# Stick-breaking attention: causal masks added ahead of the logits, and one pair of squares held behind an exponential

## The chip, the cores and the metric

The kernel runs on one core of one Trainium2 chip. The metric is the device time of one execution in microseconds (us), as the median of several runs. TensorE (PE in the profile) multiplies matrices, with its weight loads shown apart as PEld; VectorE is DVE, ScalarE is ACT, GpSimd is POOL, SyncE is SP.

## The reference

Four layers work on 256 tokens of 1024 features. Each adds a token mixer and then a squared-ReLU MLP to the residual, both on an RMS-normed input. The mixers are retention (layers 0 and 3), a convolution module (layer 1) and stick-breaking attention (layer 2). Only the last is touched by the change. Cut to what matters:

```python
q, k, v = split(xn @ w_in, 3)               # 16 heads of 64; q and k are RMS-normed per head
for b0 in range(0, s, SB_BLOCK):            # two query blocks of 128
    kend = b0 + SB_BLOCK
    z = einsum('bhqd,bhkd->bhqk', q[:, :, b0:kend], k[:, :, :kend]) * scale
    mask = s_idx[None, :] < t_idx[:, None]  # strictly causal
    log_1mb = where(mask, log_sigmoid(-z), 0.0)
    log_w = log_sigmoid(z) + cumsum(log_1mb, reverse=True) - log_1mb
    a = where(mask, exp(log_w), 0.0)
    outs.append(einsum('bhqk,bhkd->bhqd', a, v[:, :, :kend]))
y = concatenate(outs) @ w_out
```

## The kernel before

Weights stream from memory all the time. Each unit of 128x1024 numbers is split into a rounded high part (`wh`, a cast on ScalarE, line 350) and the rest (`wl`, a subtraction on VectorE, line 357), and products are summed from high and low parts in PSUM. Most of the kernel is a long row of such matmuls.

In the attention layer (`stick`), the 16 heads go in four blocks of four heads. TensorE's order is written out by hand in the string `SB_ORDER`, one short code for a step; the digit that follows is the block:

- `p` (`proj`): a quarter of the block's q and k projection, 12 matmuls of 512 columns (lines 918 to 920); `r`: the row norms; `v` (`values`): a quarter of a v projection, of the same shape.
- `n` (`norm`): per-head norms. ScalarE squares the two projected tiles out of PSUM (line 1372), VectorE sums them (line 1374), takes an inverse root (lines 384 to 395) and scales the tiles (line 1384).
- `u` and `t` (`trans`): four TensorE transposes of q, or of k (line 1394), into one PSUM tile `pt`, which ScalarE copies out (line 1399; for q also two copies of half of the rows, line 1406).
- `l` (`logits`): three PSUM tiles z2, z0, z1. Four matmuls for z2 (line 1420; keys of the second half against queries of the second half), the mask of z2 (line 1427), four matmuls for z0 and z1 (line 1433; their operands lie on 64 rows), then the masks of z0 and z1 (also line 1427). A mask is a matmul of an identity with a matrix that holds -1e30 in the places that are cut off, so it is added in PSUM.
- `s` (`soft`): per tile, absolute value, exponential and logarithm on ScalarE (lines 1445 to 1447), then three operations on VectorE (lines 1448 to 1451).
- `w` (`weights`): `w02` stands for block 0, tile z2. Suffix sums are added to the tile by TensorE (lines 1458 and 1462), and ScalarE takes the exponential of the tile (line 1464). That is the last reader of the tile.
- `m` (`mix`): the attention weights against v.

The small PSUM tiles (the `pt` of every transpose step, and z2, z0, z1) share a pool of four banks, `mis`. A step that wants a bank waits until an earlier tile's last reader is done; TensorE takes its steps strictly in the written order, so such a wait holds up everything behind it.

The part of the order that matters here is:

```python
"p00 p01 r p02 p03 p10 n0 p11 p12 p13 u0 t0 p20 n1 l0 s0 p21 p22 w02 p23 n2 w00 u1 t1 p30 l1 p31 p32 s1"
" w01 w12 p33 w10 u2 t2 w11 v00 n3 l2 s2 v01 v02 w22 v03 u3 t3 w20 v10 l3 v11 s3 w21 v12 w32 v13 w31 w30"
```

Only TensorE keeps this order. The orders of ScalarE, VectorE and GpSimd within the layer are laid out by a planner at build time, which lists the instructions by its own estimates of time and urgency; each engine then runs its list from first to last.

Of the kernel before, what the change touches and what calls it, by code (L numbers as in the profile page):

```python
# [2 lines left out]

# [8 lines left out]
AF = mybir.ActivationFunctionType  # L12
# [3 lines left out]
P = 128  # L16
D = 1024
S = 256
# [220 lines left out]
def v3(ap, a, b):  # L239
    return ap.rearrange("p (a b) -> p a b", a=a, b=b)  # L240


class Trunk:
# [1097 lines left out]
    def stick(self, j, nxt):  # L1341
        nc = self.nc
        self.table("natural_log_exp_and_others")
        kw = dict(skip_group_check=True)
        Ur, m1r, idr, negr = (self.cp.tile([P, P], F32R, name=f"{k}r", tag=f"{k}r") for k in ("U", "m1", "id", "neg"))
        for t, key in ((Ur, "U"), (m1r, "m1"), (idr, "id"), (negr, "neg")):
            nc.vector.tensor_copy(t, self.c(key, P))
        G = {}
# [17 lines left out]
        def norm(b):  # L1366
            pss = G["p", b]

            m = self.col(16, "qkm")
            for t in range(2):  # L1370
                sq = self.tmp()
                nc.scalar.activation(out=sq, in_=pss[t], func=AF.Square)
                ss = self.col(8, f"sbs{t}")
                nc.vector.tensor_reduce(out=ss, in_=v3(sq, 8, DH), op=ALU.add, axis=AX.X)
                nc.vector.tensor_scalar(
                    out=m[:, t * 8 : t * 8 + 8], in0=ss, scalar1=G["r64"][:, t : t + 1], scalar2=EPS,
                    op0=ALU.mult, op1=ALU.add,
                )
            rs = self.rsqrt(m, 16, "qk")
            f = self.col(16, "sbf")  # L1380
            nc.vector.tensor_mul(v3(f, 4, 4), v3(rs, 4, 4), G["rr"].unsqueeze(2).to_broadcast([P, 4, 4]))
            for t in range(2):
                sc = self.tmp()
                nc.vector.tensor_mul(
                    v3(sc, 8, DH), v3(pss[t], 8, DH), f[:, t * 8 : t * 8 + 8].unsqueeze(2).to_broadcast([P, 8, DH])
                )
                G["sc", b, t] = sc
# [23 lines left out]
        def logits(b):  # L1411


            z2, z0, z1 = self.mis(), self.mis(), self.mis()
            zb = G["z", b] = [z0, z1, z2]
            kT, qT = G["k", b], G["q", b]
            for e in range(2):
                for pr in range(2):
                    o = (2 * e + pr) * P
                    nc.tensor.matmul(  # L1420
                        zb[2][:, o : o + P], kT[:, pr * S + P : (pr + 1) * S], G["f", b][:, o : o + P],
                        start=o == 0, stop=False, **kw,
                    )

            def mask(z):
                n = z.shape[1]
                nc.tensor.matmul(z, idr, negr.unsqueeze(1).to_broadcast([P, n, P]), start=False, stop=True, **kw)

            mask(v3(zb[2], 4, P))
            for pr in range(2):  # L1430
                for e in range(2):
                    r = slice(e * DH, (e + 1) * DH)
                    nc.tensor.matmul(
                        zb[e][:, pr * S : (pr + 1) * S], kT[r, pr * S : pr * S + P], qT[r, pr * S : (pr + 1) * S],
                        start=pr == 0, stop=False, **kw,
                    )
            for e in range(2):
                mask(v3(zb[e], 2, S)[:, :, :P])

        def soft(b):  # L1440

# [12 lines left out]
        def weights(b, i):  # L1454

            zb = G["z", b]
            for x in G["l", b, i]:
                nc.tensor.matmul(zb[i], Ur, x, start=False, stop=True, **kw)  # L1458
            if i < 2:
                o = v3(zb[i], 2, S)[:, :, P:]  # L1460
                for x in G["l", b, 2]:
                    nc.tensor.matmul(o, m1r, v3(x[:, i * S : (i + 1) * S], 2, P), start=False, stop=True, **kw)
            G["A", b, i] = self.bigt()
            nc.scalar.activation(out=G["A", b, i], in_=zb[i], func=AF.Exp)

        def values(cb, kb):
            if kb == 0:
# [9 lines left out]
        def mix(b):  # L1477
# [15 lines left out]
        G["y"] = []  # L1493
        table = {
            "p": proj, "r": rnorm, "n": norm, "u": lambda b: trans(b, 0), "t": trans, "l": logits, "s": soft, "w": weights, "v": values, "m": mix
        }
        def go(steps):
# [62 lines left out]
```

## Time and profile before

| what | value |
| --- | --- |
| median of 3 runs | 1343.08 us (1341.48 to 1344.0) |
| span of the profiled execution | 1340.3 us |
| PE busy | 1330.8 us, 99% of the span |
| DVE, ACT, POOL busy | 984.0, 781.3, 134.0 us |
| PE clock granted | 9 in all 40 slices (90% or more); 1.00 in each stretch from 640 to 800 us |
| attention layer's blocks | about 668 to 756 us of the span |

The profile gives the profiled execution's span and no time of its own beside that; the span is 2.8 us below the median of the runs and 1.2 us below the fastest of them. In a timeline row the columns are the start, the length, the engine, the source line, the operation, the output and input tiles, the shapes and the number of merged instructions; the bracket names idle time ahead of it and what ended it. Matmul lengths overlap, since matmuls are pipelined: the distance between two starts is what one costs.

### The profile page before, as it was taken

How to read it: one execution, taken by the hardware profiler on the slowest of the kernel's cores; microseconds unless marked ns; L12 is line 12 of the kernel's file. 1: busy time of each engine (PE TensorE's matmuls, PEld its weight loads, DVE VectorE, ACT ScalarE, POOL GpSimd, SP SyncE). 2: the span in 40 equal slices, each digit the busy share in tenths (PEclk: the TensorE clock that was granted, in tenths of full speed). 3: DMA queues.
4: the chain of work that ended last, by engine and by line, in shares of the span. 5: the costliest groups of instructions: out<-in, count | busy, mean ns of one | idle time of the engine just before them, and what ended most of it. 6: DMA issues, size and time to landing. Idle time of an engine off the chain costs nothing.

```text
span 1340.3 us, 20902 instructions
## 1 busy us (share of the span) xinstructions
PE 1330.8 (99%) x8285; PEld 1170.4 (87%) x8285; DVE 984.0 (73%) x1642; ACT 781.3 (58%) x1205; POOL 134.0 (10%) x123
## 2 busy tenths in 40 slices
PE   9999999999999999999999999999999999999998
PEld 7988888888999998888878898888888888988886
DVE  6977769775688698765687587755697777788643
ACT  7555546664457477744578577744565555555442
POOL 3200002000169210000100010000120000100000
PEclk9999999999999999999999999999999999999999
DMA  7555555555545645555453345555555454555551
GB/s 283 210 184 190 187 181 197 189 188 189 188 159 145 219 170 203 190 192 192 172 183 126 126 166 190 192 190 194 177 181 187 174 188 173 189 189 189 204 188 63
DMA packets 41586, 244.56 MB, mean 182 GB/s; under 512 B 4624, under 2 KB 9104, under 8 KB 14096
## 3 DMA queue, kind: packets, MB, share of 16 engines
q1 hardware_dynamic: 40768, 240.86, 50.7%
q10 hardware_dynamic: 720, 2.36, 0.5%
q8 instruction: 65, 1.06, 0.3%
q14 instruction: 33, 0.27, 0.1%
HBM read 241.27 MB, written 1.93 MB: 181 GB/s over the span
## 4 chain that ended last, share of the span: by engine, by line
PE 99%; DMA 0%; ACT 0%; DVE 0%; issue 0%; SPq 0%
PE acc L524 34%; PE acc L520 18%; PE acc L683 6%; PE acc L918 6%; PE acc L920 6%; PE acc L919 6%; PE acc L504 4%; PE acc L505 4%; PE acc L506 4%; PE acc L1087 1%; PE acc L1220 1%; PE mis L809 1%; PE mis L870 1%; PE mis L400 0%; PE mis L1458 0%; PE acc L585 0%
## 5 line engine op out<-in xcount | busy, mean ns | idle before, releaser
L357 DVE TENSOR_TENSOR wl<-raw,wh 128x1024 fp32r<-128x1024 f32 (+1 forms) x440 | 546.5, 1247 | 242.8 <-ACT wh L350 236.4
L350 ACT CAST wh<-raw 128x1024 fp32r<-128x1024 f32 (+1 forms) x440 | 456.5, 1042 | 353.1 <-PE acc L524 164.8
L524 PE MATMUL acc<-z,wh 128*128 128x512 f32 x1120 | 387.4, 392 | 0.0
L520 PE MATMUL acc<-z,wl 128*128 128x256 f32 x1120 | 310.2, 281 | 0.0
L524 PE MATMUL acc<-big,wh 128*128 128x512 f32 x864 | 298.8, 392 | 0.0
L524 PEld LDWEIGHTS acc<-z,wh 128*128 128x128 f32 x1120 | 208.3, 187 | 44.7
L520 PE MATMUL acc<-big,wl 128*128 128x256 f32 x864 | 238.5, 280 | 0.5 <-DVE t L568 0.5
L520 PEld LDWEIGHTS acc<-z,wl 128*128 128x128 f32 x1120 | 211.1, 189 | 1.7
L524 PEld LDWEIGHTS acc<-big,wh 128*128 128x128 f32 x864 | 161.0, 187 | 34.8
L520 PEld LDWEIGHTS acc<-big,wl 128*128 128x128 f32 x864 | 162.4, 189 | 2.3 <-DVE t L568 1.3
L918 PE MATMUL acc<-wh,z 128*128 128x512 f32 x352 | 138.0, 392 | 0.0
L920 PE MATMUL acc<-wh,z 128*128 128x512 f32 x352 | 137.3, 390 | 0.0
L919 PE MATMUL acc<-wl,z 128*128 128x512 f32 x352 | 137.2, 390 | 0.0
L455 POOL TENSOR_TENSOR t<-t,t 128x512 f32<-128x512 f32 x23 | 36.2, 1573 | 893.7 <-ACT t L450 850.6
L567 ACT COPY t<-acc 128x256 f32<-128x256 f32 x176 | 61.8, 373 | 100.6 <-PE acc L524 99.3
L568 DVE TENSOR_TENSOR t<-acc,t 128x256 f32<-128x256 f32 x176 | 69.1, 421 | 34.9 <-ACT t L567 34.8
L683 PE MATMUL acc<-wh,big 128*128 128x512 f32 x256 | 79.3, 390 | 0.0
L920 PEld LDWEIGHTS acc<-wh,z 128*128 128x128 f32 x352 | 66.1, 188 | 14.7 <-issue 0.8
L918 PEld LDWEIGHTS acc<-wh,z 128*128 128x128 f32 x352 | 66.1, 188 | 14.1 <-issue 0.8
L919 PEld LDWEIGHTS acc<-wl,z 128*128 128x128 f32 x352 | 66.1, 188 | 13.1
L504 PE MATMUL acc<-z,wh 128*128 128x256 f32 x256 | 72.5, 284 | 0.0
L505 PE MATMUL acc<-z,wh 128*128 128x256 f32 x256 | 72.4, 283 | 0.0
(259 smaller groups left out, 1813.0 us busy)
## 6 DMA issues: line engine op xcount, KB each, us to landing
raw<-in_w SPq DMA_DIRECT2D x214, 1024.0 KB, 4.8
raw<-in_w SPq DMA_DIRECT2D x8, 512.0 KB, 8.9
big<-in_gn SPq DMA_DIRECT2D x16, 256.0 KB, 5.2
raw<-hd SPq DMA_DIRECT2D x8, 263.0 KB, 4.8
raw<-hd SPq DMA_DIRECT2D x8, 131.5 KB, 3.6
x<-in_x SPq DMA_DIRECT2D x4, 256.0 KB, 6.3
wh<-in_w ACTq DMA_DIRECT2D x2, 512.0 KB, 6.4
wl<-in_w ACTq DMA_DIRECT2D x2, 512.0 KB, 8.5
```

The source lines that it names most:

```text
L350: nc.scalar.copy(hi[:, s], src[:, s])
L357: self.nc.vector.tensor_sub(lo[:, s], src[:, s], hi[:, s])
L504: nc.tensor.matmul(o, wh[:, kk, cs], ah, start=st, stop=False, **kw)
L505: nc.tensor.matmul(o, wh[:, kk, cs], al, start=False, stop=False, **kw)
L520: mm = nc.tensor.matmul(ps[m][:, :S], wl[:, kk, cs], a[:, :S], start=first and kk == 0, stop=False, **kw)
L524: nc.tensor.matmul(ps[m], wh[:, kk, cs], a, start=False, stop=last and kk == 3, **kw)
L567: nc.scalar.copy(o[:, s], ps[m][:, S:])
L568: nc.vector.tensor_add(o[:, s], ps[m][:, :S], o[:, s])
L683: self.tc.keep_in_program_order(nc.tensor.matmul(ps[t], l, r[:, kk], start=False, stop=kb * 2 + kk == 31 and n == 2, **kw))
L918: nc.tensor.matmul(ps[t], zh[:, s], wh[:, kk], start=k == 0, stop=False, skip_group_check=True)
L919: nc.tensor.matmul(ps[t], zh[:, s], wl[:, kk], start=False, stop=False, skip_group_check=True)
L920: nc.tensor.matmul(ps[t], zl[:, s], wh[:, kk], start=False, stop=k == 7, skip_group_check=True)
```

## The change

Two edits in the attention layer. In `logits`, the three mask matmuls of a block come first and open their PSUM banks (`start=True`), and the eight logit matmuls are added to them; before, the logits came first and the masks closed the groups. In `norm`, for block 2 alone, the two squares carry an ordering edge: they are placed on ScalarE behind the latest exponential that `weights` has traced. With the written order that is the one of `w02`. The edge is an order on one engine; it adds no wait on another engine.

```diff
@@ norm
             for t in range(2):
                 sq = self.tmp()
-                nc.scalar.activation(out=sq, in_=pss[t], func=AF.Square)
+                with self.tc.issue_after(G["e"]) if b == 2 else nullcontext():
+                    nc.scalar.activation(out=sq, in_=pss[t], func=AF.Square)
@@ logits
+            def mask(z):
+                n = z.shape[1]
+                nc.tensor.matmul(z, idr, negr.unsqueeze(1).to_broadcast([P, n, P]), start=True, stop=False, **kw)
+
+            mask(v3(z2, 4, P))
+            for e in range(2):
+                mask(v3(zb[e], 2, S)[:, :, :P])
             for e in range(2):
                 for pr in range(2):
...
-                        start=o == 0, stop=False, **kw,
+                        start=False, stop=False, **kw,
                     )
-
-            def mask(z):
-                n = z.shape[1]
-                nc.tensor.matmul(z, idr, negr.unsqueeze(1).to_broadcast([P, n, P]), start=False, stop=True, **kw)
-
-            mask(v3(zb[2], 4, P))
             for pr in range(2):
                 for e in range(2):
...
-                        start=pr == 0, stop=False, **kw,
+                        start=False, stop=False, **kw,
                     )
-            for e in range(2):
-                mask(v3(zb[e], 2, S)[:, :, :P])
@@ weights
-            nc.scalar.activation(out=G["A", b, i], in_=zb[i], func=AF.Exp)
+            G["e"] = nc.scalar.activation(out=G["A", b, i], in_=zb[i], func=AF.Exp).ins
```

More of the change, by code (lines that the diff above doesn't have):

```diff
@@ L1 @@
 import numpy as np
-from contextlib import ExitStack
+from contextlib import ExitStack, nullcontext
 import concourse.bass as bass
```

## The prediction

> **What bounds the kernel now.** I read the page first: its parts 1, 2 and 4.
>
> ```profile
> span 1340.3 us, 20902 instructions
> PE 1330.8 (99%) x8285; PEld 1170.4 (87%) x8285; DVE 984.0 (73%) x1642; ACT 781.3 (58%) x1205; POOL 134.0 (10%) x123
> ...
> PE 99%; DMA 0%; ACT 0%; DVE 0%; issue 0%; SPq 0%
> ```
>
> TensorE is busy for 1330.8 of 1340.3 us, and the chain that ends last is TensorE for 99%. So a change is worth what it takes from TensorE's own row of instructions, or from the 9.5 us in which TensorE stands still. Next I asked for what TensorE waits for, over the whole execution (us in total, times, longest us).
>
> ```profile
> PE mis L292 <- POOL t L270: 1.3, 1, 1.3
> PE mis L1394 <- ACT big L1464: 1.0, 1, 1.0
> PE acc L585 <- ACT wh L350: 0.6, 1, 0.6
> PE acc L520 <- DVE t L568: 0.5, 2, 0.2
> ```
>
> Only one wait lies in the attention layer: a transpose (line 1394) waits once, 1.0 us, for an exponential of line 1464. The timeline shows its place. Here are TensorE's transposes of block 1, the wait, and the stall-free pair of block 0 for comparison:
>
> ```profile
> 684.05 1.03 PE L1394 MATMUL mis<-cst,t 128*128 128x128 f32 x8
> 684.84 0.47 PE L918 MATMUL acc<-wh,z 128*128 128x512 f32 x1
> 685.15 0.39 PE L919 MATMUL acc<-wl,z 128*128 128x512 f32 x1
> ...
> 695.76 0.61 PE L1458 MATMUL mis<-big,Ur 128*128 128x512 f32 x2
> ...
> 699.62 0.60 PE L1394 MATMUL mis<-cst,t 128*128 128x128 f32 x4
> 701.21 0.66 PE L1394 MATMUL mis<-cst,t 128*128 128x128 f32 x4 [0.99 <-ACT big L1464]
> 701.63 0.47 PE L918 MATMUL acc<-wh,z 128*128 128x512 f32 x1
> ```
>
> Four transposes (u1) run at 699.62; the next four (t1) start only at 701.21. The chain of waits tells why, and ScalarE's own timeline shows what it did before:
>
> ```profile
> 699.13 0.60 ACT t L1372
> 699.73 0.93 ACT wh L350
> 700.66 0.51 ACT big L1464
> ...
> 701.21 0.66 PE mis L1394 x4
> ```
>
> ```profile
> 696.91 0.62 ACT L1447 ACTIVATE t<-t 128x512 f32<-128x512 f32 x1
> 698.45 1.28 ACT L1372 ACTIVATE t<-acc 128x512 f32<-128x512 f32 x2 [0.91 <-PE acc L920]
> 699.62 1.04 ACT L350 CAST wh<-raw 128x1024 fp32r<-128x1024 f32 x1
> 700.56 1.09 ACT L1464 ACTIVATE big<-mis 128x512 f32<-128x512 f32 x2
> 701.52 0.70 ACT L1399 ACTIVATE big<-mis,prm 128x512 f32<-128x512 f32 x1
> 702.09 0.95 ACT L1406 ACTIVATE big<-mis,prm 64x256 f32<-64x256 f32 x2
> 703.07 0.69 ACT L1399 ACTIVATE big<-mis,prm 128x512 f32<-128x512 f32 x1
> ```
>
> The pair at 700.56 is the exponentials of w02 and w00. The one of w02 had its input since TensorE finished line 1458 at 695.76 + 0.61 = 696.37, yet it stands behind the two squares of block 2 and a weight cast. The squares themselves waited 0.91 us for TensorE, so ScalarE stood idle from 697.53 to 698.45 with that exponential ready. TensorE went on 0.65 us into the pair, just as the first of the two was done; the second ends at 701.65, too late to be the releaser.
>
> **The change part by part. The edge.** Both squares of block 2 now stand behind the exponential of w02. In place of the 0.91 us of idleness there is one exponential; the pair takes 1.09 us and its first member about 0.60 of it, so it runs from about 697.53 to 698.13 and the squares start at 698.45 as before. The edge adds no cross-engine wait: the exponential needs w02, which TensorE runs ahead of the projection that the squares need. Behind the squares nothing becomes late; their block is transposed (u2) much later than its scaling ends:
>
> ```profile
> 704.62 1.29 DVE L1384 TENSOR_TENSOR t<-acc,sbf 128x512 f32<-128x512 f32 x2
> ...
> 717.14 1.04 PE L1394 MATMUL mis<-cst,t 128*128 128x128 f32 x8
> ```
>
> That is 11.2 us of cover from 705.91 to 717.14. The bank of z2 is then free at about 698.2, before u1 begins, and t1 follows u1 without a gap. Block 0 gives the price of eight transposes in a row: 684.84 - 684.05 = 0.79 us. Block 1 took 701.63 - 699.62 = 2.01 us. The stall is worth 2.01 - 0.79 = 1.22 us; the bracket says 0.99, since it counts from the modelled end of the last transpose. I take 1.2 and keep 1.0 as the other end.
>
> What is late next is l1, which wants the copies of q and k out of PSUM.
>
> ```profile
> 704.48 1.05 PE L1420 MATMUL mis<-big,big 128*128 128x128 f32 x8
> ...
> 704.67 1.05 ACT L350 CAST wh<-raw 128x1024 fp32r<-128x1024 f32 x1 [0.92 <-PE acc L920]
> ```
>
> TensorE reaches l1 at 704.48 - 1.2 = 703.28. ScalarE has one exponential fewer behind the cast, 701.65 - 701.16 = 0.49 us, so k is copied by 703.76 - 0.49 = 703.27. Logits first would just meet it. Masks first put three matmuls of z2, z0, z1 in front (some 0.23 + 2 x 0.12 = 0.47 us by the rates below); they need no q or k, only banks, and the last bank, that of t1, is wanted at about 703.28 + 0.35 = 703.63. So the stall does not come back there, by a margin of about 0.35 us. After l1 the same chain of ScalarE is started by TensorE's progress (the 0.92 above, "PE acc L920"), so it moves ahead with it.
>
> **The masks.** No matmul is added or removed, only moved. Block 0 in TensorE's and the weight loads' timelines:
>
> ```profile
> 687.67 1.05 PE L1420 MATMUL mis<-big,big 128*128 128x128 f32 x8
> 688.48 0.48 PE L1427 MATMUL mis<-negr,idr 128*128 128x512 f32 x1
> 688.89 1.13 PE L1433 MATMUL mis<-big,big 64*128 64x256 f32 x8
> 688.89 0.73 PEld L1433 LDWEIGHTS mis<-big,big 64*128 64x128 f32 x8 [0.24 <-issue]
> 689.95 0.30 PEld L1427 LDWEIGHTS mis<-negr,idr 128*128 128x128 f32 x2 [0.33 <-issue]
> 689.95 0.50 PE L1427 MATMUL mis<-negr,idr 128*128 128x256 f32 x2
> 690.29 0.39 PE L918 MATMUL acc<-wh,z 128*128 128x512 f32 x1
> 690.52 0.39 PE L919 MATMUL acc<-wl,z 128*128 128x512 f32 x1
> ```
>
> Start to start, the steady 512-column matmul costs 690.52 - 690.29 = 0.23, so a 256-column one about 0.12 (an estimate, half of it). The z2 mask costs 688.89 - 688.48 = 0.41, 0.18 too much; the pair of masks 690.29 - 689.95 = 0.34, 0.10 too much. Part of that is the first rounded-type (fp32r) matmul behind plain fp32 ones: after the transposes it costs 685.15 - 684.84 = 0.31, 0.08 too much. The rest goes with the weight loads that stood idle for "issue", at the borders between 128-row and 64-row operands. A block now has two entries from fp32 to fp32r (z2's mask, the mask pair) and two row borders (into and out of line 1433). Afterwards it has one entry (the first projection matmul behind line 1433) and still two borders: into line 1433 from line 1420, and out of it into the projection. So I take one entry saved in each block, 4 x 0.08 = 0.3 us. Best case, both excesses go: 4 x 0.28 = 1.1 us gained. Worst case, no entry is saved and a border is dearer, by 0.33 - 0.24 = 0.09 as the two idle loads differ: 4 x 0.09 = 0.4 us lost. My value is nearest to the row of the transposes, which shows the entry alone.
>
> [...]
>
> **The sum.** -1.2 - 0.3 = -1.5 us, against a span of 1340.3: 1338.8. The median of the runs lies 2.8 us above the span, for what is around the profiled stretch and for the spread of runs; I subtract from the median: 1343.08 - 1.5 = 1341.6 us, 0.11% less. A difference of 0.2% (2.7 us) is about what a measurement of this kernel can tell from no change; the three runs alone lie 2.5 us apart.
>
> **The rivals.** *The masks are worth nothing.* If what they cost too much goes by the row borders alone, still two a block, only the stall's 1.2 us is gained: 1341.9. For it: the idle weight loads at both borders. Against: the 0.08 us behind the transposes, where no border of rows is.
>
> *The wait is another's.* If the bank that t1 got was freed by the exponential of w00, which could be first in the merged pair at 700.56, the new order frees it at the same 701.16 (squares, cast, exponential stay one after another) and only the masks' 0.3 us is left: 1342.8. For it: the merged row does not tell the two apart. Against: w02 had its input 3.4 us earlier (w00 runs just ahead of u1 at 699.62). This would be the case in which the edge does nothing.
>
> *The wait moves.* If ScalarE's list is laid out anew so that one more cast (1.04 us) goes ahead of the copies for t1, the margin of 0.35 us at l1 turns into a wait of about 0.7 us: -1.5 + 0.7 gives 1342.3. For it: ScalarE is nearly full here, and the orders of all engines but TensorE are planned again. Against: the cast is itself started by a weight tile that TensorE frees.
>
> *Slower: the copies come late at every logits step.* The masks want three banks at once at the head of each block, and banks are freed by ScalarE's copies and exponentials. The margins are thin at all four blocks, here at block 3:
>
> ```profile
> 736.59 0.60 ACT L1464 ACTIVATE big<-mis 128x512 f32<-128x512 f32 x1
> 737.06 1.05 PE L1420 MATMUL mis<-big,big 128*128 128x128 f32 x8
> ```
>
> That exponential frees its bank at 737.19, 0.13 us after the block begins; today only its third bank is wanted, 1.2 us in, and after the change 0.35 us in. If in each block one 1.05 us operation of ScalarE is planned ahead of the last release, each loses up to 1.05 us: 4 x 1.05 = 4.2 us against a gain of 1.5, 1345.8. It decides as soon as the four lose over 1.5 us together, 0.4 us a block. Against: the present margins at blocks 1 and 3 still hold by 0.35 and 0.2 us, and the order of the pool's tiles is the same.
>
> *Faster by over 0.2%.* With a new plan, other standstills could go as well. For it: 9.5 us of standing still. Against: the waits above name only 1.1 us of it outside the attention layer and the start (0.6 + 0.5), so even with both gone and the masks' best case it is -1.2 - 1.1 - 1.1 = -3.4, 1339.7.
>
> [...]
>
> **How the numbers follow.** My forecast has 0.38, masks worth nothing 0.20, another's wait 0.12, the moved wait 0.13, slower through late banks 0.08, the large gain 0.09. The first four all end within 0.2%. For the spread of runs I move some of the forecast to the faster side: faster by over 0.2% 0.14, within 0.2% 0.79, slower by over 0.2% 0.07. The likeliest case alone spans the bounds of its terms: from 1343.08 - 1.2 - 1.1 = 1340.8 to 1343.08 - 1.0 + 0.4 = 1342.5. The range of 8 in 10 takes in all the smaller rivals and most of the spread of the runs (1.6 us below their median, 0.9 above): low 1341.6 - 2.8 = 1338.8, high 1342.8 + 1.7 = 1344.5.
>
> **What would show it right or wrong.** Right: no wait of line 1394 for line 1464; one exponential ahead of the squares of block 2 and one behind the cast; the transposes of u1 and t1 as one row of eight taking 0.8 us; a block's first mask at 0.23 us behind the projection, and line 1433 beginning straight behind line 1420. Wrong: a wait of line 1427 for a bank, or of line 1420 for k; the row borders costing more than 0.28 us a block; TensorE's waits elsewhere changed by more than 1 us, which would mean that the plan outside this layer has moved.

## The result: 1.9 us slower, and the profile after

The changed kernel takes 1344.12 us (median of 21 runs, 1342.94 to 1345.41) against 1342.23 us before (21 runs, 1341.3 to 1344.14). The ratio is 1.0012, with a 95% interval of 1.0007 to 1.0018: slower, by 0.9 to 2.4 us. The forecast was 1.5 us less.

The span and busy times of the page of after, and what TensorE waits for in the attention layer (660 to 760 us), in the columns used before:

```profile
span 1341.7 us, 20901 instructions
PE 1330.0 (99%) x8285; PEld 1169.6 (87%) x8285; DVE 984.2 (73%) x1642; ACT 780.8 (58%) x1205; POOL 137.3 (10%) x123
```

```profile
PE mis L1395 <- ACT big L1465: 1.9, 2, 1.4
```

The same work is done, in a span 1.4 us longer. Where one wait of 1.0 us stood, there are now two, 1.9 us in all. (Lines behind the edits are numbered one higher: 1395 is the transpose, 1465 the last exponential, 1373 the squares; 1421, 1429 and 1436 are masks, z2's logits, z0's and z1's logits.) TensorE's timeline of after shows the places:

```profile
699.25 0.60 PE L1395 MATMUL mis<-cst,t 128*128 128x128 f32 x4
700.37 0.66 PE L1395 MATMUL mis<-cst,t 128*128 128x128 f32 x4 [0.51 <-ACT big L1465]
703.63 0.68 PE L1421 MATMUL mis<-negr,idr 128*128 128x512 f32 x3
...
716.11 0.40 PE L1463 MATMUL mis<-big,m1r 128*128 128x256 f32 x2
717.94 1.14 PE L1395 MATMUL mis<-cst,t 128*128 128x128 f32 x8 [1.43 <-ACT big L1465]
```

At t1 a wait of 0.51 us is left, and a new one of 1.43 us stands at u2, the transposes of block 2, which before ran at 717.14 with no wait at all. ScalarE's timeline of after explains both. First the place at t1:

```profile
696.55 0.62 ACT L1448 ACTIVATE t<-t 128x512 f32<-128x512 f32 x1
698.77 1.05 ACT L350 CAST wh<-raw 128x1024 fp32r<-128x1024 f32 x1 [1.59 <-PE acc L920]
699.72 0.59 ACT L1465 ACTIVATE big<-mis 128x512 f32<-128x512 f32 x1
700.21 1.08 ACT L1373 ACTIVATE t<-acc 128x512 f32<-128x512 f32 x2
701.16 0.61 ACT L1465 ACTIVATE big<-mis 128x512 f32<-128x512 f32 x1
```

The exponential of w02 does stand ahead of the squares. But a weight cast stands ahead of the exponential, and it waits for TensorE's projection to end (1.59 us, line 920): it needs a buffer that the last of these matmuls frees. It is the cast for the first quarter of v (`v00`), five units further on, since the weights have five buffers. So an exponential that was ready at 695.39 + 0.62 = 696.01 (line 1459, w02) starts at 699.72. It frees its bank at 700.31, and t1 starts at 700.37, 1.12 us behind u1's start rather than 1.59 before; without a wait it would be about 0.4 (an estimate: half of the 684.48 - 683.69 = 0.79 us that block 0's eight transposes take). Now the place at u2, before and then after:

```profile
712.76 1.05 ACT L350 CAST wh<-raw 128x1024 fp32r<-128x1024 f32 x1 [0.47 <-PE acc L920]
713.72 1.08 ACT L1464 ACTIVATE big<-mis 128x512 f32<-128x512 f32 x2
715.97 1.28 ACT L1372 ACTIVATE t<-acc 128x512 f32<-128x512 f32 x2 [1.17 <-PE acc L920]
```

```profile
713.58 0.63 ACT L1448 ACTIVATE t<-t 128x512 f32<-128x512 f32 x1
715.17 1.28 ACT L1373 ACTIVATE t<-acc 128x512 f32<-128x512 f32 x2 [0.96 <-PE acc L920]
716.35 1.04 ACT L350 CAST wh<-raw 128x1024 fp32r<-128x1024 f32 x1
717.28 1.58 ACT L1465 ACTIVATE big<-mis 128x512 f32<-128x512 f32 x3
718.72 1.29 ACT L1400 ACTIVATE big<-mis,prm 128x512 f32<-128x512 f32 x2
```

Before, the exponentials of w01 and w12 ran at 713.72, ahead of the squares of block 3. Now they stand behind those squares and a cast, at 717.28, though w01 and w12 ended at 713.1. They free the banks that u2 wants; the first is done at about 717.88, and u2 starts at 717.94. This is the pattern that the edge was to remove at block 2, come back at block 3, one cast and two squares long.

Last, the masks. Block 0 of after, in TensorE's timeline:

```profile
687.31 0.62 PE L1421 MATMUL mis<-negr,idr 128*128 128x512 f32 x3
687.77 1.05 PE L1429 MATMUL mis<-big,big 128*128 128x128 f32 x8
688.75 1.14 PE L1436 MATMUL mis<-big,big 64*128 64x256 f32 x8
689.82 0.50 PE L918 MATMUL acc<-wh,z 128*128 128x512 f32 x1
690.16 0.39 PE L919 MATMUL acc<-wl,z 128*128 128x512 f32 x1
```

The masks run at their steady rate, 687.77 - 687.31 = 0.46 us for three. But the logits of z2 (line 1429), which cost 0.81 before, now cost 0.98, and the first projection matmul behind line 1436 costs 0.34 rather than 0.23. To the second projection matmul the block takes 690.16 - 687.31 = 2.85 us; before it took 690.52 - 687.67 = 2.85. Nothing is won.

A good measure of the whole is the stretch of TensorE from the first transpose of block 0 to the first matmul of the output projection (line 504). It leaves out the first 680 us, which differ by up to 2.6 us between profiled executions. Each stretch is of one execution:

| kernel | from | to | stretch, us | against before |
| --- | --- | --- | --- | --- |
| before | 684.05 | 753.31 | 69.26 | |
| after | 683.69 | 754.21 | 70.52 | +1.26 |

Its parts: u1 and t1 took 2.01 before and take 700.78 - 699.25 = 1.53 now, with the projection behind them at 700.78 (-0.48); from the line 1463 of w10 to the end of u2 and t2 +1.70; masks 0.0; and 0.06 at l1, where the three masks take 0.52 rather than 0.46. The sum is +1.28.

### The profile page after: what moved, and what is told of

Read it like the earlier page. It is cut to its first block, busy times and chain, and to the rows that moved or that the text cites. A ratio compares the mean times of both kernels' runs of the same rounds, so it can differ in the third digit from the quotient of the medians.

```text
span 1341.7 us, 20901 instructions
## 1 busy us (share of the span) xinstructions
PE 1330.0 (99%) x8285; PEld 1169.6 (87%) x8285; DVE 984.2 (73%) x1642; ACT 780.8 (58%) x1205; POOL 137.3 (10%) x123
## 4 chain that ended last, share of the span: by engine, by line
PE 98%; DMA 1%; ACT 0%; SPq 0%; DVE 0%; issue 0%
PE acc L524 34%; PE acc L520 18%; PE acc L683 6%; PE acc L918 6%; PE acc L920 6%; PE acc L919 6%; PE acc L504 4%; PE acc L506 4%; PE acc L505 4%; PE acc L1087 1%; PE acc L1220 1%; DMA raw<-in_w 1%; PE mis L809 1%; PE mis L870 1%; PE mis L400 0%; PE mis L1459 0%
## 5 line engine op out<-in xcount | busy, mean ns | idle before, releaser
L520 PE MATMUL acc<-z,wl 128*128 128x256 f32 x1120 | 310.3, 281 | 0.0
L506 PE MATMUL acc<-z,wl 128*128 128x256 f32 x256 | 72.3, 283 | 0.7 <-DVE wl L357 0.7
L504 PE MATMUL acc<-z,wh 128*128 128x256 f32 x256 | 72.5, 284 | 0.0
```

Of the source, the lines that this page charges most:

```text
L504: nc.tensor.matmul(o, wh[:, kk, cs], ah, start=st, stop=False, **kw)
L506: nc.tensor.matmul(o, wl[:, kk, cs], ah, start=False, stop=en, **kw)
L520: mm = nc.tensor.matmul(ps[m][:, :S], wl[:, kk, cs], a[:, :S], start=first and kk == 0, stop=False, **kw)
```

## The experiments

Theory A: the edge lays out ScalarE's list anew, and the exponentials that free banks come late. Theory B: the masks at the head cost the time. Each kernel below was profiled; ratios are against the kernel before on the same chip.

**masks_only**: the edge is left out, the masks are first.

```diff
-                with self.tc.issue_after(G["e"]) if b == 2 else nullcontext():
-                    nc.scalar.activation(out=sq, in_=pss[t], func=AF.Square)
+                nc.scalar.activation(out=sq, in_=pss[t], func=AF.Square)
```

> The masks come first, without the ordering edge. Theory A (the loss comes from where the edge puts ScalarE's exponentials; the masks are worth nothing): ScalarE's list is as before, the one wait of 1.0 us at t1 stays, none comes at u2, the time is that of before within 0.5 us (ratio 0.9997 to 1.0004). Theory B (the loss comes from the masks, which want three banks at once and move the borders between row sizes): 1 to 2 us slower than before (ratio 1.0008 to 1.0015), with waits at the masks.

**edge_only**: the kernel before with the edge alone.

```diff
-                nc.scalar.activation(out=sq, in_=pss[t], func=AF.Square)
+                with self.tc.issue_after(G["e"]) if b == 2 else nullcontext():
+                    nc.scalar.activation(out=sq, in_=pss[t], func=AF.Square)
...
-            nc.scalar.activation(out=G["A", b, i], in_=zb[i], func=AF.Exp)
+            G["e"] = nc.scalar.activation(out=G["A", b, i], in_=zb[i], func=AF.Exp).ins
```

> The ordering edge on the squares of block 2, with the logits first as before. Theory A: as the changed kernel: a wait of about 0.5 us at t1 and one of about 1.4 us at u2, 1.0 to 1.9 us slower than before (ratio 1.0008 to 1.0014). Theory B: no wait at u2 and 0.5 us or more faster than before (ratio below 0.9997).

Measured: masks_only 1341.77 us, ratio 0.9996 (0.9987 to 1.0005); edge_only 1344.61 us, ratio 1.0015 (1.0006 to 1.0024). TensorE's waits in the layer, of masks_only and then of edge_only:

```profile
PE mis L1394 <- ACT big L1464: 1.0, 1, 1.0
```

```profile
PE mis L1395 <- ACT big L1465: 1.9, 2, 1.4
PE mis L1421 <- ACT big L1400: 0.2, 1, 0.2
```

Theory A holds and B falls. With the masks alone ScalarE's order of work is that of before, the wait is that of before, and the stretch is 69.20 us (683.88 to 753.08), 0.06 below before. With the edge alone both waits of the changed kernel are there, and the stretch is 70.94 us (684.93 to 755.87). It is 0.42 us longer than the changed kernel's, since l1 now waits for the copies of block 1 (line 1400; with the logits first, line 1421 is z2's logits): there the masks at the head do cover something.

**two_edges**: the same remedy for block 3.

```diff
-                with self.tc.issue_after(G["e"]) if b == 2 else nullcontext():
+                with self.tc.issue_after(G["e", 0, 2] if b == 2 else G["e", 1, 2]) if b > 1 else nullcontext():
...
-            G["e"] = nc.scalar.activation(out=G["A", b, i], in_=zb[i], func=AF.Exp).ins
+            G["e", b, i] = nc.scalar.activation(out=G["A", b, i], in_=zb[i], func=AF.Exp).ins
```

> The changed kernel, and the squares of block 3 held behind the exponential of w12 in the same way. Theory A: the exponentials of w01 and w12 run ahead of those squares again, so the wait at u2 falls from 1.4 us to 0.6 or less, and with the 0.5 us left at t1 the time is within 0.6 us of before (ratio 0.9996 to 1.0004), over 0.8 us below the changed kernel. Theory B: as slow as the changed kernel (ratio 1.0008 or more).

Measured: 1343.56 us, ratio 1.0007 (0.9999 to 1.0016), stretch 70.06 us (684.42 to 754.48), 0.80 over before and 0.46 below the changed kernel. The gain was half of what I expected, and it rests on the traces: the run times alone can't tell this kernel from the one before or from the changed one. ScalarE's timeline and TensorE's row at u2:

```profile
716.62 1.05 ACT L350 CAST wh<-raw 128x1024 fp32r<-128x1024 f32 x1 [1.64 <-PE acc L920]
717.57 1.08 ACT L1465 ACTIVATE big<-mis 128x512 f32<-128x512 f32 x2
718.54 1.09 ACT L1373 ACTIVATE t<-acc 128x512 f32<-128x512 f32 x2
```

```profile
718.21 1.14 PE L1395 MATMUL mis<-cst,t 128*128 128x128 f32 x8 [0.95 <-ACT big L1465]
```

The exponentials are ahead of the squares, as asked, and again a cast that waits for TensorE (1.64 us) is put ahead of the exponentials. The edge orders two instructions and says nothing of a third.

**two_edges_cast**: on top of two_edges, that third instruction is ordered too, at block 2: the cast of `v00` is held behind the exponential of w02.

```diff
-            w = self.unit(("sb_w_in", j, "a", kb, 2 * D + cb * 512))
+            with self.tc.issue_after(G["e", 0, 2]) if cb == kb == 0 else nullcontext():
+                w = self.unit(("sb_w_in", j, "a", kb, 2 * D + cb * 512))
```

> As two_edges, and the cast of the first v unit (which waits for the last matmul of the projection) is held behind the exponential of w02 as well, so that the exponential runs as soon as w02 is done. Theory A: neither the wait at t1 nor the one at u2 is left, eight transposes take 0.8 us at both places, and the time is 0.8 to 1.4 us below before (ratio 0.9989 to 0.9995); that is the gain that was forecast for the edge. Theory B: no faster than before.

**one_edge_cast**: the changed kernel with this edge on the cast, and none at block 3.

> The changed kernel with one edge more: the cast of the first v unit is held behind the exponential of w02; the squares of block 3 are left free. Theory A1 (the whole loss goes back to that cast, which the new list puts ahead of the exponential of w02 and which waits for the projection's last matmul; the order at u2 follows from it): no wait at t1, none at u2, the attention stage 1.2 us (0.9 to 1.5) shorter than before, ratio 0.9986 to 0.9996. Theory A2 (the order at u2 needs its own edge): the wait at u2 stays at 0.9 us or more and the time is within 0.6 us of before.

Measured: two_edges_cast 1341.06 us, ratio 0.9991 (0.9983 to 1.0000); one_edge_cast 1341.1 us, ratio 0.9992 (0.9983 to 1.0001). ScalarE's timeline of two_edges_cast, and TensorE's transposes of one_edge_cast:

```profile
699.19 0.62 ACT L1448 ACTIVATE t<-t 128x512 f32<-128x512 f32 x1
699.72 0.58 ACT L1465 ACTIVATE big<-mis 128x512 f32<-128x512 f32 x1
700.72 1.28 ACT L1373 ACTIVATE t<-acc 128x512 f32<-128x512 f32 x2 [0.43 <-PE acc L920]
```

```profile
699.54 1.04 PE L1395 MATMUL mis<-cst,t 128*128 128x128 f32 x8
...
715.89 1.04 PE L1395 MATMUL mis<-cst,t 128*128 128x128 f32 x8
```

This is the picture that was forecast for the edge alone: the exponential in ScalarE's idle time, then the squares, and eight transposes in one row at both places. The stretches are 68.09 us (686.32 to 754.41) and 68.08 us (683.98 to 752.06), 1.17 and 1.18 below before, where 1.2 was forecast for the edge. The lists of ScalarE at both places are the same in these two kernels, and their stretches agree within 0.01 us. By their ratios both are about 0.2% (2.7 us) below the changed kernel, and the intervals do not overlap (1.0000 and 1.0001 at most against 1.0007 at least); against the kernel before, each interval ends at no change, and the traces are the firmer evidence. Theory A1 holds: the order at u2 needs no edge of its own. It went wrong with the cast, and went back with it.

**cast_only**: masks first, the edge on the cast, none on the squares.

> Masks first and that one cast held behind the exponential of w02; no edge on the squares at all. Theory A1: the exponential of w02 comes right behind the two squares, 0.93 us earlier than before, so the wait at t1 shrinks from 1.2 to about 0.25 us (eight transposes with the wait in 1.0 to 1.1 us rather than 2.0), none comes at u2, and the stage is 0.8 to 1.0 us shorter than before (ratio 0.9988 to 0.9998). Rival: without the edge on the squares the wait at t1 stays at 0.8 us or more.

Measured: 1341.91 us, ratio 0.9992 (0.9983 to 1.0001), stretch 68.36 us (684.17 to 752.53), 0.90 below before. ScalarE's timeline and TensorE's at t1:

```profile
698.57 1.28 ACT L1372 ACTIVATE t<-acc 128x512 f32<-128x512 f32 x2 [0.91 <-PE acc L920]
699.75 1.08 ACT L1464 ACTIVATE big<-mis 128x512 f32<-128x512 f32 x2
```

```profile
699.74 1.31 PE L1394 MATMUL mis<-cst,t 128*128 128x128 f32 x8
```

Three quarters of the gain come from the cast alone, without the edge on the squares.

**two_edges_cast_lf**: as two_edges_cast, logits first.

> As two_edges_cast, with the logits first as before the change. Theory C (masks first are worth nothing by themselves, but cover the copies of q and k where TensorE comes early): TensorE waits 0.25 to 0.5 us at l1 for those copies, the stage is 0.2 to 0.45 us longer than that of two_edges_cast. Rival (masks first are worth nothing anywhere): no wait at l1, the stage as long as that of two_edges_cast within 0.1 us.

Measured: 1342.41 us, ratio 0.9996 (0.9988 to 1.0005), stretch 68.49 us (684.10 to 752.59), 0.40 longer than with the masks first (by the run times the two can't be told apart). The row of l1:

```profile
703.68 1.13 PE L1421 MATMUL mis<-big,big 128*128 128x128 f32 x8 [0.21 <-ACT big L1400]
```

Theory C holds: where TensorE comes early, masks at the head are worth 0.4 us at this one place, and nothing at the other three. ScalarE's list shows why the copy of k is late: the held cast now runs between the copies of q and of k (700.94, 1.05 us), so that k's copy ends at 702.85 + 0.69 = 703.54, just ahead of the logits.

**four_borders**: masks_only, with the logit matmuls in turn: two of 128 rows (line 1428), two of 64 rows (line 1434), and the same once more. The indices follow the new loop variable.

```diff
-            for e in range(2):
+            for u in range(2):
                 for pr in range(2):
-                    o = (2 * e + pr) * P
+                    o = (2 * u + pr) * P
...
-            for pr in range(2):
                 for e in range(2):
...
```

> The kernel masks_only with the logit matmuls of 128 and of 64 rows taken in turn, two and two, so that a block crosses four borders between row sizes rather than two; all eight matmuls stay fp32. Theory D (what a block costs over its steady rate is the row borders'): a block's three masks, logits and the projection behind them take 0.2 to 0.4 us more, 0.8 to 1.6 us over the four blocks. Rival (it is the entry from fp32 to fp32r, as the prediction had it): the same within 0.05 us a block.

Block 0 in TensorE's timeline:

```profile
687.52 0.62 PE L1420 MATMUL mis<-negr,idr 128*128 128x512 f32 x3
687.98 0.61 PE L1428 MATMUL mis<-big,big 128*128 128x128 f32 x4
688.52 0.70 PE L1434 MATMUL mis<-big,big 64*128 64x256 f32 x4
689.15 0.71 PE L1428 MATMUL mis<-big,big 128*128 128x128 f32 x4
689.79 0.70 PE L1434 MATMUL mis<-big,big 64*128 64x256 f32 x4
690.42 0.50 PE L918 MATMUL acc<-wh,z 128*128 128x512 f32 x1
```

From the masks to the projection it takes 690.42 - 687.52 = 2.90 us, against 690.01 - 687.50 = 2.51 in masks_only and 689.82 - 687.31 = 2.51 in the changed kernel, both with two borders. Two borders more cost 0.39 us, 0.2 each, with no change of type among them. So Theory D holds, at the upper end of what was expected: in this block a border cost 0.2 us by itself. Whether a change of type adds to it at the last border, into the projection, this run does not show. The single run's 1345.56 us says less, since ScalarE's list moved here as well: the transposes of block 3 got a new wait of 1.2 us (line 1394 waits twice for line 1463, 2.2 us in all; the other 1.00 is that of t1). Its pattern is the one above: a cast that waits 1.60 us for TensorE (734.15) now stands ahead of the exponential (735.10) that frees the bank. This list has no edge in it, so a new order of matmuls is enough to bring the pattern about.

## Why the prediction was wrong, point by point

- *The wait and its cause*: right. t1 waited for the exponential of w02, and once that runs early (one_edge_cast) the wait is gone and 1.2 us with it. The rival in which another exponential frees the bank falls: t1 now starts 0.06 us after the first of the two, with the second still 0.8 us away.
- *The edge*: this is the step that failed. "In place of the 0.91 us of idleness there is one exponential" took it that the rest of ScalarE's list stays as it is. The planner laid the list out anew, put the waiting cast ahead of the exponential, and ScalarE now stands idle for 1.59 us ahead of that cast instead of 0.91 ahead of the squares: 0.48 us gained instead of 1.2. The prediction had seen this cast only behind the squares, at 699.62. That casts wait for TensorE it did say, but as a reason against the rival "the wait moves"; it is what made the moved cast costly.
- *"After l1 the same chain of ScalarE is started by TensorE's progress, so it moves ahead with it"*: wrong at u2. The exponentials of w01 and w12 went behind the squares of block 3, for 1.7 us. The rival "the wait moves" had the mechanism, another cast ahead of what TensorE needs, but looked for it at l1 alone and priced it at 0.7 us. That was the nearest of the rivals.
- *l1*: right in kind, wrong in size. The copies come late there and the masks cover them: where TensorE comes early, l1 loses 0.4 us with the logits first, for which the prediction had "just meet it", and 0.06 with the masks first, for which it had a margin of 0.35.
- *The masks*: -0.3 us was mis-sized; it is 0.0 (-0.06 over the whole stretch in masks_only). The 0.08 us that I took for an entry into fp32r was not saved: z2's mask had cost 0.18 too much, and line 1429, which now stands ahead of the same border with no such entry, costs 0.17 more; the mask pair had cost 0.10 too much, and the matmul behind line 1436 now costs 0.11 more. So both excesses stayed with the borders. The 0.08 us behind the transposes, where no border is, stays unexplained. The rival "the masks are worth nothing" was right about the masks. What the traces show beside this is a cost of 0.2 us for each border added in four_borders, while the projection's full-row weight loads take 0.19 us each beside matmuls that start 0.23 us apart.
- *"Slower: the copies come late at every logits step"*: the right side for the wrong place. The masks lost 0.06 us at l1 and nothing elsewhere.
- *Sum*: forecast -1.2 - 0.3 = -1.5; in the traces -0.48 + 0.06 + 0.0 + 1.70 = +1.28. The medians' +1.9 (0.9 to 2.4) takes this in; whether the 0.6 us between is real stays open. The stretch behind line 504 was 0.5 us longer in this one execution (1341.7 - 754.21 = 587.49 against 1340.3 - 753.31 = 586.99), but it varies from 586.8 to 587.5 among kernels whose order there is the same.
- *The sign "TensorE's waits elsewhere changed by more than 1 us"*: it came up, but does not mean what the prediction took it for. Ahead of 640 us line 585 waits 1.1 us rather than 0.6, and line 506 waits 0.7 where it had no wait. Over the kernels of this document these two waits range from 0.3 to 1.7 and from 0 to 0.7 us, and the lists of ScalarE and VectorE outside the layer are the same in the traces of before and after.

Left open: why the planner moves the cast, and with it the order at u2. Its estimates are in no trace. The runs show only that the edge on the squares is enough to move both, and an edge on the cast enough to put both back.

## What to carry to other kernels

An ordering edge given to a planner is not an edit of one place: it settles one pair and lets every other instruction of the engine move, so look in ScalarE's list not only at the pair but at what may now come between, above all instructions that themselves wait for another engine. Where a buffer's last reader is ready and the buffer is wanted, order the waiting instruction that could block it (here a cast, 0.9 us by itself) before ordering the ones that merely follow. Before counting a saved transition, write down the whole row of borders before and after; one that only changed places was worth 0.0 us here (block 0 took 2.85 us before and after).

## What the runs showed of the hardware that I had not expected

In block 0 of four_borders a change between 128-row and 64-row operands on TensorE cost about 0.2 us (0.39 for two), nearly as much as one 512-column matmul at its steady 0.23. And in block 0 of the changed kernel three 128-row masks in a row, one of 512 columns and two of 256, cost 0.46 us: the steady 0.23 and the 0.23 of a pair of 256 columns (two matmuls of line 1463 start at 699.02, what follows them at 699.25). Each mask has its own weight load of 0.19 us (line 1421); the row took no longer for it than those rates.
